# Queries and keys of three of four head groups turned by transfers of 16-bit halves instead of by identity products

## The chip, the core and the metric

The kernel runs on one core of a Trainium2 chip as one program. The time is that of the device for one execution, in microseconds (us). Five engines take part, each with an instruction queue of its own that is worked through in order: PE (TensorE, the matrix products; the loads of its weights are listed apart as PEld), DVE (VectorE), ACT (ScalarE), POOL (GpSimd) and SP (SyncE, here only an issuer of transfers). Transfers are issued by an engine's queue (most by SP, some by ACT and POOL) and carried out by 16 DMA engines; in the profile ACTq and SPq are the rows of a queue that issues.

## What is computed

Two layers over 256 tokens of width 2048, each an attention-like mixer and a gated feed-forward part, in float32. The change lies in the first layer's mixer, differential attention:

```python
proj = h @ w_in
q, k, v = jnp.split(proj, [DA_Q_COLS, 2 * DA_Q_COLS], axis=-1)
q = partial_rope(rms_norm(q.reshape(bsz, seq, DA_HEADS, 2, DA_QK_DIM), q_norm_g), positions)
k = partial_rope(rms_norm(k.reshape(bsz, seq, DA_HEADS, 2, DA_QK_DIM), k_norm_g), positions)
...
s = jnp.einsum('bqhcd,bkhcd->bhcqk', qb, k).astype(jnp.float32) * scale
p = jax.nn.softmax(s, axis=-1)
a = p[:, :, 0] - lam * p[:, :, 1]
return jnp.einsum('bhqk,bkhd->bqhd', a.astype(v.dtype), v)
```

There are 16 heads of 2 x 64 columns for queries and keys and of 128 for values. The products for the scores need queries and keys with the features on the 128 partitions, while the projection leaves them with the tokens there: each has to be turned.

## The kernel before

**Units.** All weights stream in as units of 256 rows by 512 columns. `split_unit` issues a unit's load on SP (tile `raw`), has ACT round it to a high part (`act.copy`, line 264, tile `wh`) and DVE form the rest (`lagging`, the subtraction that gives `wl`, one unit later, by `low_parts`). Of `wh` and `wl` there are W_BUFS = 4 each. PE then makes twelve products of 128x512 for the unit (high by high, low by high, high by low; two row tiles; two blocks of 128 tokens) into the banks `mm`. `push_unit` keeps a list of units that are split and not yet multiplied, and `pop` takes the oldest and emits its products. A cast for a new unit therefore waits until the unit four before it is through PE.

**Steps.** Everything else is written as generators. After each unit `tick` calls `step_all`, which advances every generator in `active` to its next `yield`. A yield is thus a wait of one unit of program order. No engine's order is chosen at run time: what the generators emit stands in each engine's queue at that place, and an instruction that has to wait holds all that stands behind it on its engine. `tick` also starts the loads and DVE sums of another computation (`dot_job`, the second layer's modulation vectors, `raw<-raw,crow` on DVE), at a rate set per phase.

**The attention phase.** It goes from about 170 to 400 us of the span. The projection of head group hg (four heads) has the numbers n = 3 hg + 0, 1, 2 for queries, keys and values. The first six are summed up over the row tiles in `part` tiles (`partoh` for even n, `partol` for odd n), all six ending within a few units; 6 and 7 (group 2's queries and keys) are copied to `lateoh` and `lateol`, 9 and 10 (group 3's) to `qn`. `complete` starts `epilogue(nm, dst, n, src)` for queries and keys: squares on ACT (`sq`), their sums on DVE (`qss`), the root on POOL, for keys the scaling on DVE, then the rotation of 16 of each 64 columns (POOL `rt`, DVE). At its end, line 1041 on, stands the turn that is changed: for each token block four products with the identity on PE into a bank `wk`, a step later an ACT instruction (line 1046) that copies the bank to `dst` (`qT` or `kT`) and scales by the norm's gain. `EPI = 3` epilogues may be under way at a time; there are three `wk` banks.

**Attention.** `attend(hg, qb, heads)` is started from `pending` once the group's queries and keys are in `ready`, at most one every PACE = 4 steps, twelve in all: a mask product (`negm`) and the scores into `wk` banks, maxima on DVE (`mx`), exponentials on ACT (`e`, line 1127), the difference on DVE, a turn of `e` by identity products, its copy on ACT (line 1151), the products with `v` into the bank `po`, their squares on ACT (`osq`), the norm (`on`), a turn, and the split result `oh`, `ol`. The output projection follows; a `flush_steps` in it lets all generators run out.

**The same turn elsewhere.** In the second layer and in the feed-forward parts the kernel already turns float32 tiles by transfers: `halfwords` or `act.copy` puts the low and the high 16 bits of each word into separate planes, a DMA transpose of 16-bit elements turns both, and `words` (line 426) interleaves them again on ACT. In the second layer's `y_steps` (line 1991) the transposes are issued by ACT.

Of the kernel before, what the change touches and what calls it, by code (L numbers as in the profile page):

```python
# [15 lines left out]
U16 = mybir.dt.uint16  # L16
AF = mybir.ActivationFunctionType
# [18 lines left out]
N_EARLY = 6  # L36
EPI = 3
TURNED = 7
A_BUFS = 9
BLOCK_PAIRS = (1, 3, 5)  # L40
FIRST_SEVEN = 9
# [55 lines left out]
def block_kernel(ctx: ExitStack, tc: tile.TileContext, x, x_t, columns_in, ssd_columns, da_columns, c, ada_w,  # L97
# [14 lines left out]
    pe, act, dve, pool, sp = nc.tensor, nc.scalar, nc.vector, nc.gpsimd, nc.sync  # L112
# [35 lines left out]
    def bank(tag):  # L148
        return psum.tile([128, 512], F32, tag=tag, name=tag, bufs={"mm": 4, "wk": 3, "po": 1}[tag])

    def tmp(name="tmp"):
        return t2.tile([128, 512], F32, tag="t2", name=name)

    def small(n, name="sm"):
        return sm.tile([128, 8], F32, tag="sm", name=name)[:, :n]
# [16 lines left out]
    def take(what, n=1):  # L172
        while free[what] < n:
            yield
        free[what] -= n

    def give(what, n=1):
        free[what] += n
# [58 lines left out]
    def pop():  # L237
        kind, fn = fifo.popleft()
        if kind == "c":
            fn()  # L240
            return
        if waiting["u"] <= 1:
            low_parts()
        done = fn()
        waiting[kind] -= 1 if done is None else done
        if kind == "u":
            tick()
# [33 lines left out]
    def push_raw(w, row, col, fn, ring, n=512):  # L281
        while waiting["a"] >= limit["a"]:
            pop()
        raw = ring.tile([128, 1024 // n, n], F32, tag="araw", name="araw", bufs=A_BUFS)
        load["dma"] += 1460.0
# [138 lines left out]
    def words(dst, t):  # L424

        act.copy(dst.bitcast(U16).rearrange("p k (t e) -> p k t e", e=2),
                 t.rearrange("p (e k) t -> p k t e", e=2))
# [25 lines left out]
    def rstd_of(ss, n, count, name, v=None):  # L453
        v = small(n, name) if v is None else v
        pool.tensor_scalar(v, ss, 1.0 / count, EPS, op0=ALU.mult, op1=ALU.add)
        pool.tensor_tensor(v, v, neghalf[:, :n], op=ALU.pow)
        return v
# [342 lines left out]
    gcol = {"q": da_cols[:, 34:35], "k": da_cols[:, 35:36]}  # L800
# [192 lines left out]
    keys = [(0, 0), (0, 1), (0, 2), (1, 0), (1, 1), (1, 2), (2, 0), (2, 1), (2, 2), (3, 0), (3, 1), (3, 2)]  # L993
# [4 lines left out]
    def epilogue(nm, dst, n, src):  # L998


        A, Bt = tabs[nm]
        yield from take("epi")
        sqs = []
        for b in range(2):
            sq = tmp("sq")
            act.activation(sq, src[b], AF.Square)
            sqs.append(sq)
        yield
        rs = []
        for b in range(2):  # L1010
            ss = small(8, "qss")
            dve.tensor_reduce(ss, sqs[b].rearrange("p (g d) -> p g d", d=64), axis=AX.X, op=ALU.add)
            if nm == "q":
                rs.append(rstd_of(ss, 8, 64, "rq", dc.tile([128, 8], F32, name=f"rq{n}_{b}")))
            else:
                rs.append(rstd_of(ss, 8, 64, "qr"))
        if nm == "q":
            rq[keys[n][0]] = [r.rearrange("p (h c) -> p c h", c=2) for r in rs]
        yield
        if nm == "k":  # L1020
            yield
        q3 = [src[b].rearrange("p (g d) -> p g d", d=64) for b in range(2)]
        for b in range(2 if nm == "k" else 0):
            dve.tensor_tensor(q3[b], q3[b], rs[b][:, :, None].to_broadcast([128, 8, 64]), op=ALU.mult)
            yield
        rts = []
        for b in range(2):
            rt = held["dp"].tile([128, 8, 16], F32, tag="rt", name="rt", bufs=2)
            pool.tensor_tensor(rt[:, :, 0:8], q3[b][:, :, 8:16],
                               Bt[:, b, None, 0:8].to_broadcast([128, 8, 8]), op=ALU.mult)  # L1030
            pool.tensor_tensor(rt[:, :, 8:16], q3[b][:, :, 0:8],
                               Bt[:, b, None, 8:16].to_broadcast([128, 8, 8]), op=ALU.mult)
            rts.append(rt)
        yield
        for b in range(2):
            dve.tensor_tensor(q3[b][:, :, 0:16], q3[b][:, :, 0:16],
                              A[:, b, None, :].to_broadcast([128, 8, 16]), op=ALU.mult)
            dve.tensor_tensor(q3[b][:, :, 0:16], q3[b][:, :, 0:16], rts[b], op=ALU.add)
        yield
        for b in range(2):  # L1040
            yield from take("wk")
            ps = bank("wk")
            for h in range(4):
                pe.transpose(ps[:, h * 128:(h + 1) * 128], src[b][:, h * 128:(h + 1) * 128], ident)
            yield
            act.activation(dst[:, :, b * 128:(b + 1) * 128], ps.rearrange("p (h t) -> p h t", h=4),
                           AF.Copy, scale=gcol[nm])
            give("wk")
        give("epi")
        ready[n] = dst  # L1050

    def complete(n, src, in_psum):
# [24 lines left out]
        def steps(src=src):  # L1077
            while ahead():
                yield
            if i == 2:  # L1080
                v = held["dp"].tile([128, 2, 512], F32, tag="v", name="v", bufs=2)
                for b in range(2):
                    act.copy(v[:, b, :], src[b])
                ready[n] = v
            else:
                dst = held["dp"].tile([128, 4, 256], F32, tag=f"{nm}T", name=f"{nm}T", bufs=2)
                yield from epilogue(nm, dst, n, src)
# [768 lines left out]
    def conv_turned(banks, xc, g):  # L1856
        hs = [xc[:, 2 * b:2 * b + 2, :].rearrange("p k t -> p (k t)").bitcast(U16) for b in range(2)]
        for b in range(2):
            act.copy(hs[b].rearrange("p (e f) -> p e f", e=2), banks[b].bitcast(U16).rearrange("p (f e) -> p e f", e=2))
        xT = [half_tiles(y_turned(g + 1)[:, b]) for b in range(2)]  # L1860
        for _ in range(2):
            yield
        for b in range(2):
            sp.dma_start_transpose(xT[b], hs[b])
        for _ in range(3):
            yield
        for p in range(2):
            xin = tmp("xin").rearrange("p (k t) -> p k t", k=2)
            for b in range(2):
                act.copy(xin[:, :, b * 128:(b + 1) * 128].bitcast(U16).rearrange("p k (t e) -> p k t e", e=2),  # L1870
                         xT[b].rearrange("p (e k) t -> p k t e", e=2)[:, 2 * p:2 * p + 2])
            for i in range(2):
                conv_tile(xin[:, i, :], xc[:, 2 * p + i, :], 4 * g + 2 * p + i)
                yield
        act.activation(xc, xc, AF.Silu)
        yield

    def x_steps(g, banks):
        gp, h0 = S["gp"], 8 * g
        xc = gp.tile([128, 4, 256], F32, tag="xc", name="xc")  # L1880
        if g < TURNED:
            yield from conv_turned(banks, xc, g)
# [164 lines left out]
    for g in range(8):  # L2047
        bk = Banks()
        norm.push(wi, 4096 + g * 512, 512, bk, g >= TURNED)

# [111 lines left out]
```

## Time and profile before

| what | value |
| --- | --- |
| median of 3 runs (lowest, highest) | 2577.41 us (2577.4, 2578.33) |
| the profiled execution | 2578.1 us, of which the span is 2576.4 us |
| busy DVE, ACT | 2110.8 us (82%), 1507.5 us (59%) |
| granted TensorE clock, mean | 0.999 |
| DMA, mean over the span | 273 GB/s |
| identity products of `part` and late tiles and of `qn` | 48 and 16 |

The page lists busy time by engine, the share of the chain of work that ended last, and groups of equal instructions. A row of a group ends with its busy time, the mean in ns, and the idle time of its engine just before it with what ended it. A row of a timeline gives start and duration in us, engine, line, operation, output and input, and in brackets the idle time before it and the releaser. A row of the chain gives start, duration, engine and line. The time per instruction on ACT and DVE overlaps its neighbours by about 0.1 us when they follow one another: casts of 1.04 us start 0.94 us apart. The matrix products overlap more, and their cost is read from the distance of their starts.

### The profile page before, as it was taken

What the parts mean: (1) busy time and instruction counts of PE and PEld (TensorE: products, weight loads), DVE (VectorE), ACT (ScalarE), POOL (GpSimd) and SP (SyncE); (2) the same over time, 40 slices, a digit from 0 to 9 for tenths busy, and PEclk for the clock granted to TensorE, in tenths of its full rate; (3) what the DMA queues carried; (4) which work ended last, traced back from release to release, by engine and by line L of the source; (5) the groups of instructions that cost most, each with busy time, mean ns of one, the idle gap of its engine ahead of it and who ended that gap; (6) DMA issues with size and microseconds to landing.
All of it is one profiled execution on the core that took longest, in us unless ns stands there. A gap on an engine that the chain in (4) does not pass through costs nothing.

```text
span 2576.4 us, 34370 instructions
## 1 busy us (share of the span) xinstructions
PE 2551.2 (99%) x12144; PEld 2092.2 (81%) x12144; DVE 2110.8 (82%) x2955; ACT 1507.5 (59%) x2059; POOL 145.4 (6%) x225
## 2 busy tenths in 40 slices
PE   8999999999999999999999999999999999999999
PEld 5667778888888888888988888888888888888887
DVE  6779988778988898777878788888779999897675
ACT  4446654555655564446557777686566666665443
POOL 0014431000000000000000100000000000000000
PEclk9999999999999999999999999999999999999999
DMA  9987888699999869994677988878756667678884
GB/s 388 398 313 285 278 293 318 257 316 321 339 332 371 294 223 344 340 345 131 210 268 249 301 249 274 278 233 270 248 169 210 210 221 209 215 219 269 290 286 170
DMA packets 272989, 704.42 MB, mean 273 GB/s; under 512 B 101408, under 2 KB 109856, under 8 KB 271536
## 3 DMA queue, kind: packets, MB, share of 16 engines
q1 hardware_dynamic: 250960, 683.49, 76.8%
q10 hardware_dynamic: 17760, 4.43, 1.5%
q0 software_dynamic: 4096, 14.29, 1.5%
q8 instruction: 95, 1.56, 0.2%
q14 instruction: 78, 0.64, 0.1%
HBM read 680.53 MB, written 2.20 MB: 265 GB/s over the span
## 4 chain that ended last, share of the span: by engine, by line
PE 90%; DVE 4%; ACT 2%; DMA 2%; issue 1%; ACTq 0%; SPq 0%; POOL 0%; DVEq 0%; POOLq 0%
PE mm L126 62%; PE wk L126 22%; PE po L126 7%; DVE wl L126 1%; ACT wh L264 1%; DMA raw<-in_ssd_w_in 1%; DVE raw L126 1%; DMA raw<-in_ffn_w_gate_up 1%; DVE x L126 0%; DMA araw<-in_ada_w 0%; DMA raw<-in_da_w_in 0%; ACT hm L610 0%; ACTq L1991 0%; ACT e L1127 0%; DVE hm L126 0%
## 5 line engine op out<-in xcount | busy, mean ns | idle before, releaser
L264 ACT CAST wh<-raw 128x1024 fp32r<-128x1024 f32 (+3 forms) x822 | 842.2, 1037 | 744.0 <-PE mm L126 329.9
L126 DVE TENSOR_TENSOR wl<-raw,wh 128x1024 fp32r<-128x1024 f32 (+2 forms) x894 | 1043.5, 1184 | 208.8 <-ACT wh L264 207.6
L126 PE MATMUL mm<-wh,ah 128*128 128x512 f32 x2310 | 913.6, 395 | 3.1 <-ACT ah L988 1.7
L126 PE MATMUL mm<-wl,ah 128*128 128x512 f32 x2310 | 900.8, 390 | 3.0 <-DVE wl L126 3.0
L126 PE MATMUL mm<-wh,al 128*128 128x512 f32 x2310 | 901.7, 390 | 0.1
L126 PEld LDWEIGHTS mm<-wh,ah 128*128 128x128 f32 x2310 | 434.2, 188 | 108.9 <-issue 14.0
L126 PEld LDWEIGHTS mm<-wl,ah 128*128 128x128 f32 x2310 | 434.5, 188 | 96.1 <-DVE wl L126 8.5
L126 PEld LDWEIGHTS mm<-wh,al 128*128 128x128 f32 x2310 | 433.9, 188 | 94.4 <-DVE al L126 4.3
L126 DVE SCALAR_TENSOR_TENSOR raw<-raw,crow 128x1024 f32<-128x1024 f32 x320 | 389.9, 1220 | 0.0
L126 PE MATMUL wk<-wl,ah 128*128 128x512 f32 x594 | 231.8, 390 | 0.0
L126 PE MATMUL wk<-wh,al 128*128 128x512 f32 x594 | 231.3, 389 | 0.0
L126 PE MATMUL wk<-wh,ah 128*128 128x512 f32 x594 | 231.2, 389 | 0.0
L126 PEld LDWEIGHTS wk<-wl,ah 128*128 128x128 f32 x594 | 111.5, 188 | 25.5 <-DVE wl L126 2.6
L345 ACT CAST wh<-sums 128x1024 fp32r<-128x1024 f32 x72 | 75.6, 1050 | 93.8 <-PE mm L126 50.1
L126 PEld LDWEIGHTS wk<-wh,ah 128*128 128x128 f32 x594 | 111.5, 188 | 23.4
L126 PEld LDWEIGHTS wk<-wh,al 128*128 128x128 f32 x594 | 111.6, 188 | 22.8
L126 DVE TENSOR_TENSOR wl<-sums,wh 128x1024 fp32r<-128x1024 f32 x72 | 88.0, 1222 | 35.7 <-ACT wh L345 35.4
L552 POOL DMA_DIRECT2D gate_row<-grows x32 | 16.1, 511 | 1341.9 <-DVE grows L126 1341.9
L345 ACT CAST wh<-raw 128x1024 fp32r<-128x1024 f32 x72 | 59.0, 836 | 40.7 <-PE mm L126 25.0
L126 PE MATMUL po<-wh,ah 128*128 128x512 f32 x180 | 70.2, 390 | 0.0
L126 PE MATMUL po<-wh,al 128*128 128x512 f32 x180 | 70.0, 389 | 0.0
L126 PE MATMUL po<-wl,ah 128*128 128x512 f32 x180 | 70.0, 389 | 0.0
(371 smaller groups left out, 2582.9 us busy)
## 6 DMA issues: line engine op xcount, KB each, us to landing
raw<-in_ffn_w_gate_up SPq DMA_DIRECT2D x352, 512.0 KB, 4.8
raw<-in_ada_w SPq DMA_DIRECT2D x320, 512.0 KB, 5.3
raw<-in_ffn_w_down SPq DMA_DIRECT2D x176, 512.0 KB, 5.1
raw<-in_ssd_w_in SPq DMA_DIRECT2D x136, 512.0 KB, 5.7
raw<-in_da_w_in SPq DMA_DIRECT2D x90, 512.0 KB, 5.4
araw<-in_ada_w SPq DMA_DIRECT2D x64, 512.0 KB, 8.3
raw<-in_ssd_w_out SPq DMA_DIRECT2D x64, 512.0 KB, 5.0
raw<-in_da_w_out SPq DMA_DIRECT2D x32, 512.0 KB, 5.3
```

The costliest lines, as they stand in the source:

```text
L126: return fn(dst, *a, **k)
L264: act.copy(wh[:, at, :n], raw[:, at, :n])
L345: act.copy(wh[:, at, :], raw[:, at, :])
L552: pool.dma_start(gate_dram[hf][:, 32 * q:32 * q + 32], rows[o:o + 8, :])
```

## The change

For head groups 0, 1 and 2 the identity products and the copies out of the banks are gone. In their place, for each of the two token blocks: an ACT copy that separates the halves of the words, into the still unused `dst` as scratch; directly behind it a DMA transpose issued by ACT, back into the source tile; a step. Then TURN_STEPS = 3 steps, then for each block an ACT copy that puts the words together in `dst`, and one ACT instruction over the whole of `dst` (128x1024) that scales by the gain. Group 3 keeps the identity products.

```diff
+TURN_STEPS = 3
...
         yield
-        for b in range(2):
+        if keys[n][0] < 3:
+            flat = dst.rearrange("p h t -> p (h t)").bitcast(U16)
+            turned = [src[b].bitcast(U16).rearrange("p (j t) -> p j t", t=128) for b in range(2)]
+            for b in range(2):
+                h = flat[:, b * 1024:(b + 1) * 1024]
+                act.copy(h.rearrange("p (e f) -> p e f", e=2), src[b].bitcast(U16).rearrange("p (f e) -> p e f", e=2))
+                act.dma_start_transpose(turned[b], h)
+                yield
+            for _ in range(TURN_STEPS):
+                yield
+            for b in range(2):
+                words(dst[:, :, b * 128:(b + 1) * 128], turned[b])
+                yield
+            act.activation(dst, dst, AF.Copy, scale=gcol[nm])
+        for b in range(2 if keys[n][0] == 3 else 0):
             yield from take("wk")
             ps = bank("wk")
             for h in range(4):
```

The change adds lines ahead of these, so that line 264 becomes 265, 426 becomes 427, and the added copy, transpose and scaling are lines 1046, 1047 and 1054.

The first place is ACT's queue where the first epilogues end (groups 0 and 1). Before: `qT<-wk` and `kT<-wk` are the copies out of the banks, `CAST wh<-raw` the casts of units.

```order
L1083 COPY v<-partol 128x512 x2
L1046 ACTIVATE qT<-wk,da_cols 128x4x128
L264 CAST wh<-raw 128x1024
L1046 ACTIVATE qT<-wk,da_cols 128x4x128
L1006 ACTIVATE sq<-partoh 128x512 x2
L264 CAST wh<-raw 128x1024
L1046 ACTIVATE kT<-wk,da_cols 128x4x128
L1046 ACTIVATE qT<-wk,da_cols 128x4x128
L264 CAST wh<-raw 128x1024
L1046 ACTIVATE kT<-wk,da_cols 128x4x128
L1046 ACTIVATE qT<-wk,da_cols 128x4x128
L264 CAST wh<-raw 128x1024
```

After, at the same place of ACT's queue, from the second transpose of group 0's queries on; ahead of it stand the copy of `v` and one copy of halves, `qT<-partoh`.

```order
L1047 DMA_TRANSPOSE partoh<-qT 128x8x128
L265 CAST wh<-raw 128x1024
L1046 COPY kT<-partol 128x1024
L1047 DMA_TRANSPOSE partol<-kT 128x8x128
L1046 COPY qT<-partol 128x1024
L1047 DMA_TRANSPOSE partol<-qT 128x8x128
L265 CAST wh<-raw 128x1024
L1046 COPY kT<-partol 128x1024
L1047 DMA_TRANSPOSE partol<-kT 128x8x128
L1046 COPY qT<-partol 128x1024
L1047 DMA_TRANSPOSE partol<-qT 128x8x128
L265 CAST wh<-raw 128x1024 x2
```

Where one or two short copies stood between two casts, there are now two copies and two issued transposes; the squares of group 1's keys (`sq<-partoh`) and the first exponentials have moved behind this piece.

The second place is ACT's queue at group 2's queries and keys. Before, with `e` the exponentials of an earlier group:

```order
L1127 ACTIVATE e_2553,sums<-wk,mx,rq_0_1868 128x128 x4
L1127 ACTIVATE e_2560,sums<-wk,mx,rq_0_1868 128x128 x4
L264 CAST wh<-raw 128x1024
L1064 COPY lateol<-mm 128x512 x2
L1006 ACTIVATE sq<-lateol 128x512 x2
L1046 ACTIVATE qT<-wk,da_cols 128x4x128
L264 CAST wh<-raw 128x1024
L1046 ACTIVATE qT<-wk,da_cols 128x4x128
L1179 ACTIVATE osq,oss<-po 128x128 x4
L264 CAST wh<-raw 128x1024
L1151 COPY e_2553<-wk 128x512
L264 CAST wh<-raw 128x1024
```

After, at the same exponentials, with the transposes of queries and keys between the casts:

```order
L1047 DMA_TRANSPOSE lateoh<-qT 128x8x128
L1142 ACTIVATE e_2662,sums<-wk,mx,rq_0_1868 128x128 x4
L1142 ACTIVATE e_2669,sums<-wk,mx,rq_0_1868 128x128 x4
L265 CAST wh<-raw 128x1024
L1046 COPY qT<-lateoh 128x1024
L1047 DMA_TRANSPOSE lateoh<-qT 128x8x128
L265 CAST wh<-raw 128x1024
L1194 ACTIVATE osq,oss<-po 128x128 x4
L1046 COPY kT<-lateol 128x1024
L1047 DMA_TRANSPOSE lateol<-kT 128x8x128
L265 CAST wh<-raw 128x1024
L1046 COPY kT<-lateol 128x1024
```

Here too each transpose stands directly behind the copy that makes its source, and ahead of a cast or of the exponentials.

The third place is PE's queue at the scores of group 1's last heads. Before, four identity products of `lateol` (group 2's keys) stand ahead of the mask and the scores:

```order
L126 MATMUL mm<-wl,ah 128x512
L126 MATMUL mm<-wh,al 128x512
L126 MATMUL wk<-ident,lateol 128x128 x4
L126 LDWEIGHTS identb
L126 MATMUL wk<-negm,identb 128x2x128
L126 LDWEIGHTS identb
L126 MATMUL wk<-negm,identb 128x2x128
L126 MATMUL wk<-kT,qT 128x256 x4
L126 MATMUL mm<-wh,ah 128x512
```

After, at the same scores, the last product of a unit is followed by the mask:

```order
L127 MATMUL mm<-wl,ah 128x512
L127 MATMUL mm<-wh,al 128x512
L127 LDWEIGHTS identb
L127 MATMUL wk<-negm,identb 128x2x128
L127 LDWEIGHTS identb
L127 MATMUL wk<-negm,identb 128x2x128
L127 MATMUL wk<-kT,qT 128x256 x4
L127 MATMUL mm<-wh,ah 128x512
```

Such groups of four (two of them directly behind one another twice) leave PE's queue twelve times. The first scores of all have moved five units later in PE's queue. SP's queue holds the same transfers in the same order, and by the end of the attention phase the queues of PE, DVE and POOL are the same again.

## Prediction

> **What bounds the kernel now.** First the page: the span, the busy shares and the chain that ended last.
>
> ```profile
> span 2576.4 us, 34370 instructions
> PE 2551.2 (99%) x12144; PEld 2092.2 (81%) x12144; DVE 2110.8 (82%) x2955; ACT 1507.5 (59%) x2059; POOL 145.4 (6%) x225
> PE 90%; DVE 4%; ACT 2%; DMA 2%; issue 1%; ACTq 0%; SPq 0%; POOL 0%; DVEq 0%; POOLq 0%
> ```
>
> PE bounds the whole, so a microsecond taken out of its queue counts in full if nothing else becomes late. Whether it does is a question of the attention phase alone; so next the windows of that phase (busy us of PE, PEld, DVE, ACT, POOL, then clock, DMA share, GB/s).
>
> ```profile
> 200.00:220.00 20.00, 18.77 (x103) 14.85 (x102) 18.79 (x37) 15.43 (x33) 9.25 (x15) 1.00 0.66 213
> 220.00:240.00 20.00, 20.00 (x106) 15.59 (x105) 17.37 (x33) 12.43 (x29) 4.38 (x8) 1.00 0.98 378
> 240.00:260.00 20.00, 20.00 (x113) 16.32 (x112) 19.08 (x39) 12.09 (x33) 8.72 (x11) 1.00 0.89 314
> 260.00:280.00 20.00, 20.00 (x107) 16.27 (x106) 18.92 (x37) 15.53 (x40) 12.86 (x15) 1.00 0.75 258
> 280.00:300.00 20.00, 18.90 (x110) 15.06 (x109) 19.47 (x36) 10.54 (x19) 6.74 (x10) 1.00 0.88 287
> ```
>
> Three resources are near their end at once here. DVE is busy for 93.6 of 100 us, the DMA engines for 0.83 on average, ACT for 66.0 of 100. ACT's 34 idle us look like room, so I ask what they are (the waits of ACT from 190 to 420: total, times, longest).
>
> ```profile
> ACT e L1127 <- DVE mx L126: 25.5, 10, 3.6
> ACT wh L264 <- PE mm L126: 24.4, 17, 1.8
> ```
>
> The second row is true room: ACT has cast a unit as far ahead as the four buffers allow, and waits for PE. The first is not: the exponentials stand at the head of the queue and the casts behind them.
>
> **The change, part by part.** *PE's products.* The chain gives their real cost.
>
> ```profile
> 206.07 0.87 PE wk L126 x8
> 209.68 1.54 PE wk L126 x18
> 219.63 0.44 PE wk L126 x4
> 347.23 13.62 PE mm L126 x60
> ```
>
> Four identity products hold PE for 0.44 us, eight for 0.87; the 48 that go are twelve such fours: 12 x 0.44 = **5.3 us less**. A unit of twelve products takes 13.62 / 5 = 2.72 us.
>
> *PE's waits.* Three of the products that go now wait (bracket: idle before it).
>
> ```profile
> 194.22 0.63 PE L126 MATMUL wk<-ident,partoh 128*128 128x128 f32 x4 [1.54 <-DVE partoh L126]
> 201.12 0.63 PE L126 MATMUL wk<-ident,partol 128*128 128x128 f32 x4 [0.31 <-DVE partol L126]
> 202.67 0.63 PE L126 MATMUL wk<-ident,partol 128*128 128x128 f32 x4 [0.92 <-ACT wh L264]
> ```
>
> These 2.8 us go from the products, but DVE was the late one, and its work stays. After them PE next waits for the low parts of units, which DVE makes between the rotations:
>
> ```profile
> 202.97 2.35 DVE L126 TENSOR_TENSOR wl<-raw,wh 128x1024 fp32r<-128x1024 f32 x2
> ```
>
> The first of these two ends at about 204.2 and no step of DVE ahead of it changes. So the unit that began at 206.7 before begins at 204.2, whatever PE saves ahead of it: DVE gives PE 2.5 us there and keeps the rest. Its row and that of the unit four later, needed below:
>
> ```profile
> 206.70 0.48 PE L126 MATMUL mm<-wh,ah 128*128 128x512 f32 x1
> 219.82 0.48 PE L126 MATMUL mm<-wh,ah 128*128 128x512 f32 x1
> ```
>
> *ACT, the price.* Here are the durations of what is added and removed, by groups of the same form (busy, mean ns), and two places where ACT issues a transpose with nothing to do meanwhile.
>
> ```profile
> L264 ACT CAST wh<-raw 128x1024 fp32r<-128x1024 f32 (+3 forms) x822 | 842.2, 1037 | 744.0 <-PE mm L126 329.9
> L1981 ACT COPY yT<-xsd 128x1024 uint16<-128x1024 uint16 x14 | 14.6, 1041 | 2.8 <-DVE xsd L126 2.8
> L426 ACT COPY yw<-yT 128x1024 uint16<-128x1024 uint16 x16 | 17.9, 1165 | 0.0
> L1934 ACT ACTIVATE abc<-abc 128x1024 f32<-128x1024 f32 x8 | 8.5, 1057 | 0.0
> L1046 ACT ACTIVATE qT<-wk,da_cols 128x512 f32<-128x512 f32 x8 | 5.6, 706 | 0.0
> ...
> 1690.25 1.31 ACTq L1991 DMA_TRANSPOSE yT<-yT  x1
> 1691.62 0.40 ACT L1917 ACTIVATE abc<-abc,acum 128x128 f32<-128x128 f32 x1 [0.75 <-ACT ah L406]
> 1739.96 1.28 ACTq L1991 DMA_TRANSPOSE yT<-sz  x1
> 1741.34 1.05 ACT L264 CAST wh<-raw 128x1024 fp32r<-128x1024 f32 x1 [0.82 <-PE mm L126]
> 1741.42 1.96 ACTq L1991 DMA_TRANSPOSE yT<-sz  x1
> 1743.47 2.00 ACT L264 CAST wh<-raw 128x1024 fp32r<-128x1024 f32 x2 [1.08 <-issue]
> ```
>
> The transpose is no busy time in the windows, but what follows in the queue starts only when its row ends: 1690.25 + 1.31, and the next begins at 1691.62. In the second layer most of that is hidden, since ACT's queue issues while earlier work still runs. Here it isn't: the transpose stands directly behind the copy that makes its source, so ACT must first be empty. A copy with its transpose costs ACT 1.04 + 1.37 = 2.41 us. In all ACT gets 12 x 2.41 + 12 x 1.17 + 6 x 1.06 = 49.3 us and loses 12 x 0.70 = 8.4: **41 us more**, against 34 idle in the 100 us where nearly all of it falls.
>
> *ACT, the first piece.* I follow the queue of the change from the copies of `v`.
>
> ```profile
> 199.89 1.22 ACT L1083 COPY v<-partol 128x512 f32<-128x512 f32 x2 [4.34 <-DVE partol L126]
> ```
>
> They end at 201.1 and cannot be earlier (DVE). Then, by the rows of the order: copy and transpose, cast A, two copies and transposes, cast B, two more, casts C and D. A ends at 201.1 + 2.4 + 1.0 = 204.5, B at 204.5 + 4.8 + 1.0 = 210.3, C at 216.2, D at 217.1. PE uses A's unit at 204.2 + 2.7 = 206.9. It wants B's at 209.6 and can have it, after DVE's 1.2, at 211.6: 2.0 us lost. It wants C's at 214.4 and gets it at 217.5: 3.1 lost. D's is in time, at 220.2. Before, D's unit began at 219.8, and by then PE had done the first scores (1.54) and a turn of `e` (0.44), which it still owes now. So the change is 0.4 + 2.0 = **2.4 us behind** at D, with six of the twelve fours already gone.
>
> *The rest.* Six fours remain, 2.6 us to the good. Against them ACT has in 220 to 300 another 30.5 us (the first piece's words and scalings, 10.1; six copies with transposes, 14.5; their words and scalings, 10.1; less six copies out of the banks, 4.2) and 80 - 50.6 = 29.4 idle. From nothing, if its waits shrink as it falls behind, to 11.3 lost, if four of the ten waits for `mx`, 2.55 us on average, lie in this stretch and stay (30.5 - 19.2): I take **3 us**, nearer to nothing, because a late ACT finds `mx` ready, and because DVE, which gets its gaps from ACT, has only 6.4 us of its own in the 100.
>
> *Free by cover.* The transfers themselves have time. On ACT's queue the earlier ones landed so long after issue (all rows of line 1991):
>
> ```profile
> DMA to landing us min/median/max: 3.2/5.4/12.0
> ```
>
> By the added durations, 11 us or more lie between a transpose and its words in the order. If one is late, ACT stands with casts behind it. Scores come five units later, but attention has slack until the phase ends, where the queues are alike again. One wait stays either way, or is worth 1.1 us if attention's delay dissolves it:
>
> ```profile
> 282.67 0.27 PE L126 MATMUL wk<-negm,identb 128*128 128x256 bf16 x1 [1.10 <-DVE ol L126]
> ```
>
> **Sum.** The profiled execution took 2578.1 us (span 2576.4), 0.7 above the median. 2578.1 + 2.4 - 2.6 + 3 = 2580.9, that is **2580** on the median's scale. What a measurement of this kernel can tell from no change is about 0.2%, 5.2 us: I forecast no difference, with a lean to slower.
>
> **Rivals.** *ACT keeps up and PE gets everything.* For it: ACT's 24.4 us of true room, and four buffers, 4 x 2.72 = 10.9 us deep. Then 5.3 + 2.8, up to 1.1 more: 2569 to 2572. Against it: the buffers are already empty when the first piece begins, since DVE holds `v` until 199.89, and three resources are near full.
>
> *Slower: the second transpose of a pair waits at issue.* SP's own transposes show it (start, duration):
>
> ```profile
> 643.00 1.39 SPq L421 DMA_TRANSPOSE turned<-halfwords  x1
> 645.05 3.88 SPq L421 DMA_TRANSPOSE turned<-halfwords  x1
> ```
>
> The second, 2 us behind the first, took 3.88 instead of 1.31. The same pairs stand ahead of casts B and C, where PE is late already, so each excess goes to PE in full: 2 x 2.6 = 5.1, which gives 2585; with the upper bound of the rest (8.3 more) 2594. It decides as soon as a transpose takes longer than 1.31. Against it: SP's queue also carries the weights; ACT's took 1.96 at worst in the pair above.
>
> A rule of the Trainium skill speaks for this side. The page "VectorE: DVE Perf Modes", sections "The three transpose paths" and "Rules for kernel authors", gives 390 ns for a 128x128 turn on TensorE and 1309 ns by the X-bar, and advises TensorE where PSUM will do as the destination, as it does here. Were all 48 on one path, its figures would cost 48 x 0.92 = 44 us, an estimate; the rows above (0.44 for four on PE) show that the two don't lie on one path here, so by that rule only the direction follows.
>
> *The DMA engines.* Queue 10 carried the second layer's transposes (packets, MB, share of 16 engines):
>
> ```profile
> q10 hardware_dynamic: 17760, 4.43, 1.5%
> ```
>
> 1.5% of 2576 us over 16 transposes is 2.4 us of all engines each, so twelve take 29 us where 17 of 100 are free. For it: late loads would hold the casts, at most 12 us. Against it: loads are issued ahead into seven buffers, and SP mostly waits for DVE to free them (total, times, longest):
>
> ```profile
> SPq L261 <- DVE wl L126: 1078.8, 534, 15.1
> ```
>
> I count it with the slower case.
>
> That the products do not leave PE is excluded by the order.
>
> **How the numbers follow.** No difference, 2572.3 to 2582.6: 0.48. Everything gained, below 2572.3: 0.20, because it needs nearly all of the 5.3 and 2.8. Slower than 2582.6: 0.32, because the forecast lies only 2.4 us from that edge and the unknown prices (0 to 11.3, 0 to 5.1) point that way. The range runs from 2571, a gain with little lost, to 2590, the forecast with the pairs' 5.1 and half of the rest's upper bound.
>
> **What would show it.** PE's `wk<-ident` with `part` and `late` gone, the twelve fours with them; ACT idle after each transpose by about 0.4 us beyond its copy and the row 1.3 long; PE waiting for `wl` or `wh` between 195 and 220 for some 9 us in all, against 2.8 now; D's unit near 220. If transposes take 2 us or more, the slower case holds; if ACT still waits for PE between 200 and 220, the gain does. I am wrong in kind if words wait for transfers, or if the loss lies behind 300 us.

## The result and the profile after

| what | before | after |
| --- | --- | --- |
| median (lowest to highest, runs) | 2577.77 us (2577.4 to 2579.03, 6) | 2600.7 us (2596.11 to 2607.14, 6) |
| the profiled execution (its span) | 2578.1 us (2576.4) | 2601.34 us (2599.6) |
| ratio of the times, 95% interval | | 1.0091, 1.0077 to 1.0105 |

The change costs 23 us, 0.9%. The forecast was 2580 us, in a range from 2571 to 2590; the kernel is 11 us slower than the end of that range. First the page of the changed kernel, the lines that answer to those of before (busy us by engine, and the queue that carries the transposes: packets, MB, share of 16 engines):

```profile
span 2599.6 us, 34317 instructions
PE 2554.2 (98%) x12096; PEld 2090.3 (80%) x12096; DVE 2110.9 (81%) x2955; ACT 1531.2 (59%) x2077; POOL 144.1 (6%) x225
q10 hardware_dynamic: 30432, 7.58, 2.1%
```

PE has 48 products fewer and is busy 3 us longer; ACT has grown by 24 us, and the twelve issued transposes, 16.3 us of its queue by their rows, don't count as busy. The page can't say more. The windows of the attention phase can (busy us of PE, PEld, DVE, ACT, POOL, then granted clock, DMA share, GB/s):

```profile
200.00:220.00 20.00, 15.29 (x57) 11.14 (x56) 10.00 (x17) 12.89 (x14) 2.02 (x6) 0.92 0.84 197
220.00:240.00 20.00, 17.75 (x82) 14.00 (x81) 18.53 (x36) 18.07 (x33) 8.49 (x13) 0.91 0.99 387
240.00:260.00 20.00, 20.00 (x104) 15.60 (x104) 17.61 (x31) 12.12 (x26) 2.30 (x3) 1.00 1.07 319
260.00:280.00 20.00, 16.85 (x91) 13.10 (x90) 17.46 (x33) 15.35 (x25) 14.41 (x17) 1.00 0.82 290
280.00:300.00 20.00, 19.23 (x92) 14.96 (x92) 15.58 (x32) 12.05 (x33) 5.30 (x8) 1.00 0.89 208
300.00:320.00 20.00, 12.04 (x57) 9.59 (x57) 14.68 (x28) 16.15 (x36) 5.90 (x9) 0.83 0.95 263
```

Three things differ from before. PE is empty for 4.7 us of the first window (1.2 before) and for 8.0 of the last. DVE, which was at 94%, is at 50% in the first window: it is starved, not overloaded (twice there it stands for a cast, 4.8 and 4.5 us). And the clock, 1.00 in every such window before, is 0.92, 0.91 and 0.83 in three. The first stretch of ACT's timeline (start, duration; ACTq is a row of its issuing queue) shows why DVE starves:

```profile
203.18 1.04 ACT L265 CAST wh<-raw 128x1024 fp32r<-128x1024 f32 x1 [1.43 <-PE mm L127]
204.13 1.04 ACT L1046 COPY kT<-partol 128x1024 uint16<-128x1024 uint16 x1
205.25 1.28 ACTq L1047 DMA_TRANSPOSE partol<-kT  x1
206.56 1.05 ACT L1046 COPY qT<-partol 128x1024 uint16<-128x1024 uint16 x1 [1.39 <-issue]
207.68 1.47 ACTq L1047 DMA_TRANSPOSE partol<-qT  x1
209.20 1.04 ACT L265 CAST wh<-raw 128x1024 fp32r<-128x1024 f32 x1 [1.59 <-issue]
...
214.92 1.99 ACT L265 CAST wh<-raw 128x1024 fp32r<-128x1024 f32 x2 [1.36 <-PE mm L127]
```

A copy with its transpose takes 204.13 to 206.56, 2.43 us. The names in brackets are those of waits that were over; what ACT stands for is its own transpose. Behind it PE runs out of units (timeline of PE, idle time before in brackets; the last three rows are first products of groups of three; the last one begins the unit of cast D):

```profile
197.36 0.47 PE L127 MATMUL mm<-wh,ah 128*128 128x512 f32 x1 [2.17 <-DVE partoh L127]
...
203.95 0.50 PE L127 MATMUL mm<-wl,ah 128*128 128x512 f32 x1 [0.68 <-DVE wl L127]
...
210.29 0.51 PE L127 MATMUL mm<-wh,ah 128*128 128x512 f32 x1 [0.83 <-ACT wh L265]
211.55 0.50 PE L127 MATMUL mm<-wl,ah 128*128 128x512 f32 x1 [0.75 <-DVE wl L127]
...
216.02 0.50 PE L127 MATMUL mm<-wh,ah 128*128 128x512 f32 x1 [1.68 <-ACT wh L265]
217.28 0.80 PE L127 MATMUL mm<-wl,ah 128*128 128x512 f32 x1 [0.76 <-DVE wl L127]
218.30 0.63 PE L127 MATMUL mm<-wh,ah 128*128 128x512 f32 x1
...
219.58 0.63 PE L127 MATMUL mm<-wh,ah 128*128 128x512 f32 x1
...
222.14 0.63 PE L127 MATMUL mm<-wh,ah 128*128 128x512 f32 x1
```

From 217.3 on three products take 1.28 us (218.30 to 219.58) where a unit's 2.72 us made it 0.68 before: about half speed. The second hole is near 300. One view of all engines from 289 to 310 shows its chain:

```profile
288.36 2.16 ACTq L1047 DMA_TRANSPOSE lateoh<-qT  x1
...
292.79 0.20 POOL L1196 TENSOR_TENSOR oss<-oss,r 128x4 f32<-128x4 f32 x1 [10.74 <-ACT osq L1194]
...
295.72 0.65 POOL L545 DMA_DIRECT2D gate_bias<-in_columns  x1
...
305.44 0.17 DVE L127 TENSOR_TENSOR gate_cols<-gate_cols,gate_bias 128x8 f32<-128x8 f32 x1 [5.11 <-DMA gate_bias<-in_columns]
...
308.85 1.09 PE L127 MATMUL wk<-ident,on 128*128 128x128 f32 x4 [7.96 <-DVE mx L127]
```

ACT is late with `osq` behind a transpose of 2.16 us; POOL's queue stands for it; behind that, POOL issues a transfer of 4 KB that `dot_job` needs (`gate_bias`); it lands 9.7 us later; DVE stands 5.1 us for it, and PE 8 us for DVE. None of these queues was in my sum.

### The profile page after: what moved, and what is told of

Its sections match the earlier page's. It is cut to its first block, busy times and chain, and to the rows that moved or that the text cites. A ratio compares the mean times of both kernels' runs of the same rounds, so it can differ in the third digit from the quotient of the medians.

```text
span 2599.6 us, 34317 instructions
## 1 busy us (share of the span) xinstructions
PE 2554.2 (98%) x12096; PEld 2090.3 (80%) x12096; DVE 2110.9 (81%) x2955; ACT 1531.2 (59%) x2077; POOL 144.1 (6%) x225
## 4 chain that ended last, share of the span: by engine, by line
PE 50%; ACT 1%; DMA 1%; DVE 1%; issue 0%; ACTq 0%; SPq 0%; POOL 0%; DVEq 0%
PE mm L127 32%; PE wk L127 14%; PE po L127 4%; DMA raw<-in_ssd_w_in 1%; ACT wh L265 0%; DVE wl L127 0%; ACTq L2006 0%; ACT xin L1885 0%; ACT L1926 0%; DVE raw L127 0%; ACT abc L1932 0%; ACT yw L427 0%; DVE xc L127 0%; ACT xc L1754 0%; ACT junk L465 0%
## 5 line engine op out<-in xcount | busy, mean ns | idle before, releaser
L127 PEld LDWEIGHTS mm<-wl,ah 128*128 128x128 f32 x2310 | 435.1, 188 | 101.0 <-DVE wl L127 13.2
```

Of the source, the lines that this page charges most:

```text
L127: return fn(dst, *a, **k)
```

## The experiments

All are compared with the kernel before on the same chip, with four to eleven runs of each changed kernel. "+9.5" means the difference of the two medians.

**What can be gained at all.** The products are left out and nothing replaces them.

```diff
         for b in range(2):
+            if keys[n][0] < 3:
+                yield
+                act.activation(dst[:, :, b * 128:(b + 1) * 128], src[b].rearrange("p (h t) -> p h t", h=4), AF.Copy, scale=gcol[nm])
+                continue
             yield from take("wk")
```

> The kernel before with the 48 identity products of three groups left out and nothing in their place (queries and keys are not turned; ACT scales them from their source with the same twelve activations). It shows the most that the change could give. Theory A (TensorE bounds, its products count in full and its 2.8 us of waits are mostly kept by VectorE): 2578 - 5.3 - 0.5 = 2572 us, 2570 to 2573. Rival B (VectorE and ACT set the pace of this phase): 2575 us or more.

Measured: 2577.85 us against 2578.79, **-0.9**; ratio 0.9999, interval 0.999 to 1.0007, which includes no change. Rival B: the 5.3 us are not to be had; the end of the interval leaves 2.6. Timeline of PE in this kernel:

```profile
197.45 0.47 PE L126 MATMUL mm<-wh,ah 128*128 128x512 f32 x1 [2.19 <-DVE partoh L126]
...
204.04 0.50 PE L126 MATMUL mm<-wl,ah 128*128 128x512 f32 x1 [0.64 <-DVE wl L126]
...
275.78 0.63 PE L126 MATMUL wk<-ident,on 128*128 128x128 f32 x4 [1.93 <-DVE mx L126]
```

PE reaches each of these places earlier and waits there for DVE. In the profiled execution 2.9 us of span remain of the 5.3, in the medians 0.9.

**The later place in the program.** The same kernel, with the scaling where the change has it:

```diff
             if keys[n][0] < 3:
-                yield
+                for _ in range(6 if b == 0 else 1):
+                    yield
```

> The kernel before without the 48 identity products and with nothing in their place, as in the run without a turn, but with the scaling seven steps behind the rotation, where the change has it, instead of two. No work is added to any engine. Theory A (part of the 10 us that the change costs without its transfers is the later place of queries and keys in the program, and with it of the attention): 2582 to 2590 us. Rival B (it is ACT's added work, and the place costs nothing): 2576 to 2580 us, as without a turn (2577.9).

Measured: 2582.76 against 2578.85, **+3.9**; ratio 1.0013, interval 1.0004 to 1.0022. Theory A: five steps of delay, with no work added to any engine, cost 4.8 us against the run without a turn (the two ran on different chips, each with its own kernel before, and their intervals just overlap). PE's rows where the time goes:

```profile
273.14 1.11 PE L126 MATMUL wk<-ident,e 128*128 128x128 f32 x4 [1.58 <-DVE e L126]
...
289.76 0.63 PE L126 MATMUL wk<-ident,on 128*128 128x128 f32 x4 [3.06 <-DVE mx L126]
```

The attention comes later, and the turns of `e` and `on` stand in PE's queue before DVE has made them.

**ACT's arithmetic.** The change without its transposes (copies, words and scalings stay; the words are copied from a source that needs no strides, 1.04 us each instead of 1.17).

```diff
-                act.dma_start_transpose(turned[b], h)
...
-                words(dst[:, :, b * 128:(b + 1) * 128], turned[b])
+                act.copy(dst[:, :, b * 128:(b + 1) * 128].bitcast(U16).rearrange("p k (t e) -> p k t e", e=2), src[b].bitcast(U16).rearrange("p (k t e) -> p k t e", k=4, e=2))
```

> The change without its twelve transposing transfers; the copies into halves, the copies of words and the scalings stay on ACT, so queries and keys of three groups are not turned. Theory A (what costs is the issue of the transposes on ACT's queue, 12 x 1.37 us of a blocked queue, and what it makes late): ACT's arithmetic of some 25 us fits its idle time, 2580 us or less, no wait over 3 us near 300 and no half-speed stretch. Rival B (ACT's added arithmetic is enough to make it late): 2590 us or more, with the same waits of TensorE for wh and wl between 200 and 220.

Measured: 2588.27 against 2578.79, **+9.5**; ratio 1.0037, interval 1.0025 to 1.0049. It lies between the two forecasts: the arithmetic alone is 5.6 us more than the late place, and the 13 us that are left of the change's 23 come with the transposes.

**ACT's queue held as long, without a transfer.** A second copy and a quarter of one stand where each transpose stood.

```diff
                 act.copy(h.rearrange("p (e f) -> p e f", e=2), src[b].bitcast(U16).rearrange("p (f e) -> p e f", e=2))
+                act.copy(h.rearrange("p (e f) -> p e f", e=2), src[b].bitcast(U16).rearrange("p (f e) -> p e f", e=2))
+                act.copy(h[:, 0:256].rearrange("p (e f) -> p e f", e=2), src[b].bitcast(U16)[:, 0:256].rearrange("p (f e) -> p e f", e=2))
```

> The change without its transfers, and in the place of each an ACT copy of 1.04 us and a quarter of one more (about 1.35 us, as long as a transpose's row in ACT's queue; the turning is left out). No transfer is added. Theory A (the transposes cost what they take of ACT's queue): 2588 + 12 = 2600 us, 2596 to 2604. Rival B (they cost through the DMA engines, where queue 10 takes 18% of 120 us and the weights land later): 2588 to 2593 us.

Measured: 2595.96 against 2578.85, **+17.1**; ratio 1.0068, interval 1.0055 to 1.0081. ACT's timeline shows that the copy is a fair one:

```profile
204.65 1.04 ACT L1046 COPY kT<-partol 128x1024 uint16<-128x1024 uint16 x1
205.72 1.05 ACT L1047 COPY kT<-partol 128x1024 uint16<-128x1024 uint16 x1
206.79 0.41 ACT L1048 COPY kT<-partol 128x256 uint16<-128x256 uint16 x1
207.11 1.04 ACT L1046 COPY qT<-partol 128x1024 uint16<-128x1024 uint16 x1
```

204.65 to 207.11 are 2.46 us, against 2.43 in the change. Time in ACT's queue costs 7.6 us here, without any transfer: theory A, for the larger part.

**The load on the DMA engines.** Plain transfers of 512 KB from memory to memory, issued by ACT, in place of the quarter copies.

```diff
+    scrap = {(n, b): tc.dram_tile([128, 1024], F32, name=f"scrap{n}_{b}") for n in (0, 1, 3, 4, 6, 7) for b in range(2)}
...
-                act.copy(h[:, 0:256].rearrange("p (e f) -> p e f", e=2), src[b].bitcast(U16)[:, 0:256].rearrange("p (f e) -> p e f", e=2))
+                act.dma_start(scrap[n, b], ada_rows[0, 2].unit(128 * n, b * 1024, 1024)[:, 0, :])
```

> The change without its transfers, with a second ACT copy in the place of each and, in the place of the quarter copy, a plain transfer of 512 KB from memory to memory issued by ACT at the same point (12 in all, into buffers that nothing reads; the turning is left out). ACT's queue is held about as long as with two copies and a quarter (2596 us); the DMA engines get 12 x 1.5 us of all sixteen, by what the weights of the same size take (79.1% of 120 us for 64 of them), against 1.8 us for a transpose. Theory A (what is left of the change's cost above 2596, some 5 us, is the load on the DMA engines): 2600 to 2606 us. Rival B (the load costs nothing, the rest is the issue or the wait for landing): 2593 to 2598 us.

Measured: 2592.89 against 2578.02, **+14.9**; ratio 1.0061, interval 1.0048 to 1.0075. The queues from 195 to 315 us (packets, MB, share of 16 engines), this kernel first, then the change:

```profile
q10 hardware_dynamic: 384, 6.29, 15.2%
```

```profile
q10 hardware_dynamic: 12672, 3.15, 18.3%
```

A load not far below that of the change's profile, and no cost: rival B. (In the second profile of the change, below, queue 10 had 24.5%.) It comes in 384 large packets against 12672 small ones, so what is excluded is a cost of the load as such, not one of the transposes' own packets. ACT's timeline shows that the plain issue doesn't hold ACT:

```profile
204.36 1.05 ACT L1048 COPY kT<-partol 128x1024 uint16<-128x1024 uint16 x1
204.37 0.50 ACTq L1049 DMA_DIRECT2D scrap<-in_ada_w  x1
205.31 1.04 ACT L1047 COPY qT<-partol 128x1024 uint16<-128x1024 uint16 x1
```

The next copy starts as if nothing stood between: a plain transfer of weights needs nothing of the copy ahead of it and is issued while that copy runs, where a transpose waits for its source. So each place holds the queue some 0.4 us less than with the quarter copy; that goes the way of the lower time. The change itself ran again beside it, unaltered:

> The change itself once more, beside the run with plain transfers and on the same chip. Its first six runs lay between 2596 and 2607. Theory A (there is a cost beyond the place, the arithmetic and the time in ACT's queue): 2600 us or more, 4 us or more above 2596. Rival B (there is none; 2600.7 and 2596.0 differ by the spread of the runs): 2599 us or less.

Measured: 2601.19 (2594.76 to 2604.2) against 2578.02, **+23.2**; ratio 1.0086, interval 1.0073 to 1.01. So some 6 us lie above the kernel with copies; the two intervals just overlap. Four of its rows near 300 (ACT's timeline; then, from the view of transfers issued from 285 to 320 us, the median us to landing):

```profile
295.74 4.18 ACTq L1047 DMA_TRANSPOSE lateol<-kT  x1
...
311.11 1.04 ACT L265 CAST wh<-raw 128x1024 fp32r<-128x1024 f32 x1 [4.46 <-DMA raw<-in_da_w_in]
```

```profile
lateol<-kT ACTq DMA_TRANSPOSE x2, 17.5
gate_bias<-in_columns POOLq DMA_DIRECT2D x1, 4.0 KB, 10.3
```

A transpose that takes 4.18 us to issue, two with a median of 17.5 to landing, and a transfer of 4 KB that takes 10.3. This is where the last 6 us show: from 300 to 320 us PE is empty for 8.0 us at a clock of 0.83 in the change's first profile, for 2.7 us at 0.91 in the kernel with copies. From 300 to 305 the change's DMA engines count as busy throughout and yet move 122 GB/s, against 375 before; queue 10 has 59% of their time there, for 0.20 MB. So the transposes' own packets may be what delays the rest; I have no run that takes this away.

**The small transfer behind POOL.** The change, with `gate_bias` of the first gate loaded at the start.

```diff
+    gate_b = const.tile([128, 16], F32, name="gate_b")
+    pool.dma_start(gate_b, columns_in[:, 209:225])
...
-                b = small(8, "gate_bias")
-                o = 209 + 16 * n + 8 * hf
-                pool.dma_start(b, columns_in[:, o:o + 8])
+                b = gate_b[:, 8 * hf:8 * hf + 8] if n == 0 else small(8, "gate_bias")
+                if n:
+                    pool.dma_start(b, columns_in[:, 209 + 16 * n + 8 * hf:217 + 16 * n + 8 * hf])
```

> The change, with gate_bias of the first gate loaded once at the start (one transfer of 16 columns) in place of two small transfers that GpSimd issues inside the attention phase. Theory A (late ACT holds GpSimd's queue, which issues the small transfer late, on which VectorE and then TensorE stand 8.0 us near 301): that wait goes, and the half-speed stretch behind it (about 2 us): 2601 - 10 = 2591 us, 2588 to 2594. Rival B (VectorE and ACT are late there anyway, the transfer is only what ends last): another wait of 4 us or more stands in its place, 2596 us or more.

Measured: 2601.01 against 2578.79, **+22.2**, as the change. The wait of 8 us is gone; PE's timeline has these instead:

```profile
231.58 1.31 PE L127 MATMUL wk<-kT,qT 64*128 64x128 f32 x16 [3.65 <-ACT kT L1056]
...
272.32 0.63 PE L127 MATMUL wk<-ident,on 128*128 128x128 f32 x4 [2.95 <-DVE on L127]
...
305.80 0.63 PE L127 MATMUL wk<-ident,on 128*128 128x128 f32 x4 [1.87 <-DVE mx L127]
...
314.05 0.27 PE L127 MATMUL wk<-negm,identb 128*128 128x256 bf16 x1 [3.39 <-DVE ol L127]
```

Rival B by the time, though no single wait of 4 us has come in its place: the first two were 2.25 and 1.90 us in the change's first profile, and the last is 3.82 us in its second. The most striking wait of a profile was what happened to end last; ACT and DVE were late there anyway.

**Other places for the issue.** One step of other work between copy and transpose (first diff, two lines), and SyncE as the issuer (second).

```diff
+                yield
                 act.dma_start_transpose(turned[b], h)
```

> The change with one step of other work between each copy into halves and its transpose, so that a cast can stand between them in ACT's queue. Theory A (the issue costs 1.3 us of ACT only because the transpose stands directly behind the copy that it waits for; behind a cast it is hidden under it): ACT gets back about 1 us of each of twelve, 12 us, and the time falls to 2585 to 2592 us. Rival B (the issue blocks ACT's queue for 1.25 us or more wherever it stands): within 4 us of the change, 2597 to 2605 us.

Measured: 2602.59 against 2578.79, **+23.8**: rival B. The issue still holds the queue, now also behind casts (ACT's timeline):

```profile
206.33 2.91 ACTq L1048 DMA_TRANSPOSE partoh<-qT  x1
...
209.65 2.08 ACTq L1048 DMA_TRANSPOSE partol<-qT  x1
211.82 1.05 ACT L265 CAST wh<-raw 128x1024 fp32r<-128x1024 f32 x1 [4.08 <-issue]
```

Closer together, two of the transposes take 2 to 3 us to issue, and a cast stands 4.08 us behind them. What is hidden is given back.

```diff
-                act.dma_start_transpose(turned[b], h)
+                sp.dma_start_transpose(turned[b], h)
```

> The change with the twelve transposes issued by SyncE instead of ACT; the same copies, words and scalings, the same transfers. The change without transfers took 2588.3 us, 12 us less than the change. Theory A (those 12 us are ACT's blocked queue, 12 x 1.25 us and more): they come back, 2586 to 2592 us. Rival B (they are the transfers themselves: the DMA engines carry 6336 packets of queue 10 between 195 and 235 us, and the weights come late): 2598 us or more, with ACT's casts still waiting for raw. Rival C (SyncE now stands until the copy is made, with the weights behind it): over 2603 us.

Measured: 2627.88 against 2578.49, **+49.4**: rival C. Waits from 190 to 420 us (total, times, longest):

```profile
ACT wh L265 <- DMA raw<-in_da_w_in: 60.0, 17, 6.0
DVE wl L127 <- ACT wh L265: 44.4, 14, 7.8
```

SP stands until a copy is made, and the weights stand behind it: ACT waits 60 us for them, against 19.0 in the change.

**Which group, and when.** Two kernels use transfers for a part of the groups only (`keys[n][0] < 2`, and `== 2`, in place of `< 3`).

> The change for the first two head groups only (8 of the 12 transposes, 6 of them between 195 and 215); the third group is turned by identity products as before. Theory A (the loss is spread over the pieces, about 2 us for each transpose): 2578 + 8/12 x 23 = 2593 us, 2590 to 2596. Rival B (the loss near 300, 8 us of wait and a half-speed stretch, is the third group's and the rest belongs to 195 to 240): 2589 us or less. Rival C (the crowd of six in 20 us starts it all, and what comes later is its late ACT): 2597 us or more.

> The change for the third head group only (4 of the 12 transposes, all near 280 to 300); the first two groups are turned by identity products as before. The first two alone cost 15.7 us. Theory A (the groups' losses add): 2578.5 + 23 - 15.7 = 2586 us, 2583 to 2588. Rival B (the third group loses only because ACT comes to it late from the first two): 2577 to 2581 us.

Measured: 2594.22 against 2578.49, **+15.7** for eight transposes, and 2585.25 against 2578.85, **+6.4** (ratio 1.0025, interval 1.0016 to 1.0034) for four. Theory A both times: 1.6 to 2.0 us for each transpose with what belongs to it, whichever group, and 22.1 together. Two more move the consumers:

```diff
-TURN_STEPS = 3
+TURN_STEPS = 0
```

> The change with no steps between the second transpose and the words (three in the change). Three steps more behind the scaling cost 15 us. Theory A (each step by which queries and keys come later costs time): 2590 to 2597 us, although words may wait for transfers. Rival B (the transfers take 3 to 11 us to land; ACT now stands at the words, with the casts behind them): 2603 us or more.

```diff
             act.activation(dst, dst, AF.Copy, scale=gcol[nm])
+            for _ in range(3):
+                yield
```

> The change with three more steps of other work between the scaling of turned queries or keys and the scores that use them, in the order of the program. TensorE waits 2.3 us there in the profile of the change, 3.2 and 3.7 and 7.1 in the three kernels made from it, for scaled keys. Theory A (the scores stand in TensorE's queue ahead of products that are ready): this wait goes, with the half-speed stretch behind it, 2592 to 2598 us. Rival B (TensorE would wait for casts there instead): within 3 us of the change, 2598 to 2604 us.

Measured: 2627.0 against 2578.85, **+48.2**, and 2615.49 against 2578.49, **+37.0**: rival B for the first; for the second neither, it was worse than both had it. With no steps ACT stands at the words for the transposes to land (waits from 190 to 420 us):

```profile
ACT kT L427 <- DMA partoh<-kT: 15.9, 1, 15.9
ACT qT L427 <- DMA lateoh<-qT: 9.5, 1, 9.5
ACT kT L427 <- DMA lateol<-kT: 7.3, 1, 7.3
```

With three steps more behind the scaling the wait for `kT` goes, and PE then waits 7.9 us ahead of the turn of `on`, released by ACT's `e`. Why three steps cost 14 us here, where five cost 4.8 without the added work, I have not taken apart.

**The products as filling.** The change, plus 48 products of the identity with itself. They stand where the three steps of cover stood, with two steps and the wait for a free bank in place of the three, so the words come at a somewhat other place too.

> The change, with four products of the identity with itself in the place of each four that left TensorE (48 in all, results unused, waiting for nothing but a free bank). Theory A (the half-speed stretches, 6.8 us twice in the change, come from the empty time of TensorE that these products filled; they cost about 5 us): the granted clock stays at 1.0 between 200 and 320 and the time stays within 2 us of the change or falls by up to 5: 2596 to 2602 us. Rival B (the stretches come from the waits for casts, which remain; TensorE bounds): the stretches stay and the products cost their 5.3 us, 2604 us or more.

Measured: 2609.59 against 2578.49, **+31.1**: rival B, and more. PE waits 6.12 us for `kT` at 228.89 and 3.99 for `e` at 243.94, and the clock falls all the same (0.83 from 220 to 260). Since the place of the words moved as well, the 8 us above the change are not the products' alone.

## Why the forecast was wrong

By medians, from one kernel to the next: products gone -0.9; later place +4.8 (to +3.9); ACT's arithmetic +5.6 (to +9.5); ACT's queue held for the issue +7.6 (to +17.1); what is left with real transposes +6.1 (to +23.2). The intervals of neighbours touch or overlap in the second and the last of these steps, so each size is good to some 3 to 5 us.

- **"5.3 us less" on PE: mis-sized.** 0.9 in the medians, 2.6 at the end of the interval. That PE bounds the whole was true of the page, but in this phase DVE was at 94%, as the prediction itself shows, and PE only moved up to DVE's results. I applied that reading to the 2.8 us of waits and not to the 5.3.
- **ACT's price, 2.41 us for copy and transpose, 41 us in all: right** (2.43 measured; 24 us more busy time and 16.3 us of issues make 40).
- **"The first piece": right as far as it went.** Casts A and B end at 204.2 and 210.2 (204.5 and 210.3 foreseen), C and D at 216.9 at the latest (216.2, 217.1). C's low part comes at 217.3 (217.5). From 195 to 218 PE waits 4.7 us for `wh` and `wl`, where I named 9 (6.9 with the wait for `partoh` ahead of 197.4). D's unit begins at 222.1 instead of 220.2, because the products from 217.3 on run at half speed, which I did not expect. With the 2.0 us still owed, that is 4.3 behind instead of 2.4.
- **"The rest", 3 us: the step that failed.** I set 30.5 us of added work against ACT's idle 29.4 and took almost nothing, since a late ACT would find `mx` ready. Of the 23.2 us by which the span grew, 4.3 had come about by D's unit; the other 18.9 came behind it, where my sum had 3 - 2.6 = 0.4. But a late ACT hands its lateness on: `osq` to POOL, casts to DVE, `kT` to PE. ACT's added time, arithmetic and issue together, costs 5.6 + 7.6 = 13.2 us over both pieces, where I had 2.4 and 3 with 2.6 to set off; even the upper bound of 11.3 for the rest would have given only 2589.
- **"Free by cover": half right.** No words waited for a transfer in the profiled change, and the cover of three steps was needed: without it the time is 25 us longer. But it is not free: being five steps later costs 4.8 by itself. "Attention has slack until the phase ends" was wrong.
- **The rival "the second transpose waits at issue"** exists, but elsewhere: one long issue in each profile of the change, 2.16 and 4.18 us, both near 300; in the two pairs that I named the second took 1.47 and 1.25. **The rival "DMA engines"** by load alone fell (14.9 with the load, 17.1 with copies); a transpose took 1.8 us of all engines, 18.3% of 120 us for twelve, not 2.4. That its packets delay others near 300 is not excluded.
- **The two paths' prices.** Four turns by identity products take 0.44 us of PE, and leaving all of them out gives back next to nothing; four by transfer take 2.43 us of ACT before any word is put together. By the Trainium skill, page "VectorE: DVE Perf Modes", section "Rules for kernel authors", a 128x128 turn belongs on TensorE where PSUM will do; these runs agree.
- **"Wrong in kind if the loss lies behind 300 us"**: PE's largest wait did, at 300.9 to 308.9, so by my own sign it was.

What stays open: the last 6 us are located in the profiles (near 300, where the last transposes, the weights and the small transfer land late together) and not settled; whether the stretches of half speed cost what their length says was not tested apart, since the one kernel that was to keep the clock up did not.

## What to carry to other kernels

Before work is moved off the fullest engine, leave it out altogether and measure: that ceiling, 0.9 us here and not clear of zero, decides whether any price can be paid. An engine that feeds the others has no idle time to give away where its gaps are waits in the middle of a chain; here 41 us added to its queue, the issues counted, cost 13 us, although 34 idle us stood beside them. And the longest wait in a profile need not be the cause: taking it away here only let the next one show.

## What the runs showed of the hardware

- **The clock fell without a long pause.** In the change, 0.92 and 0.91 in two windows of 20 us are 3.2 + 3.6 = 6.8 us at half speed (narrower windows show 0.50 from 217.3 to 222). They came behind waits of PE of 0.68 to 2.17 us each, 6.1 us within 21. In the kernel without the products the waits from 195 to 218 were 2.8 us, one of them 2.19, and the clock stayed at 1.00. The Trainium skill, page "TensorE: Matmul & The Clock Gate", section "HAM oscillation", gives as the rule no idle gap of PE beyond about 3.4 us; here the longest gap ahead of it was 2.17, so keeping to that rule was not enough. The second stretch of 6.8 us, near 300, began some 4.5 us into PE's wait of 8.0 and ended at 312.2, so only half of it fell on products: the two together cost at most some 5 us, an estimate from these windows.
- **A transpose holds the issuing queue.** The row was 1.24 us at least in every kernel here, and 2 to 4 us in a few cases. Another transpose under way isn't enough for that: the one at 213.63 took 1.25 us 2.4 us behind its neighbour. What sets it is not shown. A plain transfer of twice the bytes took 0.5 us.
